# Where the last two spread groups are staged, and what the buffers of the dense expert part wait for

## The chip, the cores and the metric

The kernel runs on one core of a Trainium2 chip. The metric is the device time of one execution in microseconds (us); lower is better.

## The reference, cut to what matters

One decoder layer over 1,024 tokens of width 1,024: a mixer of three branches (stick-breaking attention, sparse attention, a gated recurrence), merged and added to x; then a PEER expert network; then a final norm. The expert network, of which the change touches a part, is:

```
h    = rms_norm(x)
s    = einsum(h @ w_q, sub_keys)           # 8 heads, two sets of 128 keys
top16 of each set -> 256 sums -> top16     # 128 of 16,384 experts per token
gate = softmax(best)
out  = sum over the 128: gate * gelu(h . u[e]) * v[e]
```

## The kernel before, in words

The tokens are worked on in four parts of 256 (`PARTS`). All parts go through the mixer, the merge, the output product (`wo`, lines 928 to 941), the second norm, the key scores and the routing. The experts are then computed in one of two ways.

Parts 0 and 3 are gathered (`gather_tile`, line 1139): for each tile of 128 tokens and each of 128 choices POOL issues an indirect DMA for one row of `u` (or `v`) per token, and DVE takes the dot product (line 1151) or adds the scaled row into the tile `gacc` (line 1161). Parts 1 and 2 (`DENSE`, 512 tokens) are computed densely: every one of the 16,384 experts for every token, with a matrix of gates that is zero where an expert was not chosen.

That matrix, `d_G`, is made by the spread pieces (`spread_pieces`, line 1208). Each call of `four` takes four tokens, a quad: DVE builds one-hot tiles `hot` (lines 1219 and 1220), PE multiplies them into a PSUM bank `gb` (lines 1223 and 1224, 8 matmuls a quad, two banks), and ACT evicts the 128x512 result into a staging tile (line 1226). After four quads, a group of 16 tokens, ACT issues the write of 1 MB into `d_G` (line 1228). There are 32 groups. Groups 0 to 29 go round three staging buffers: two halves of `stages` and one tile `stage` in the pool `per`; groups 30 and 31 use `stage` too, as group 29 does. `stages` shares its buffer with the tile `h2`, into which SP loads the normed tokens of the dense part (line 1389).

The dense part goes over 128 blocks of 128 experts. `gemm1` (line 1391) loads a block of `u` transposed (`uraw`, 512 KB, in a buffer of the pool `w4`, whose four buffers the `hot` tiles use as well), splits it into two fp16 parts (ACT line 220, DVE line 221, result `us`), makes 24 matmuls `g` (line 265) and a gelu on ACT into `ge` (line 1400, a buffer with the tag `at`). It runs three blocks ahead (`LEAD`). The main loop loads `vraw` (line 1422), and for every eight blocks two gate tiles `gt` (line 1429, 1 MB each, the first from groups 0 to 15 of `d_G`, the second from groups 16 to 31), multiplies `ge` by them (line 1434), splits the product into `ac`, and adds 18 matmuls into six PSUM banks `acc` (line 1441); a seventh and eighth sum lie in SBUF (`acc7`). Between the blocks it emits the pieces of part 3 that are left (`ending`): the rest of its output product, norm, scores and routing.

Pools: `per` and `w2` (SBUF) and `ps_z`, `ps_tr`, `ps_ov` (PSUM) belong to the mixer and are closed at line 1407. `late` (vraw, vs, gt, ac, acc7) and `ps_a` (acc) are opened after that (lines 1408 and 1409) over the same bytes and banks. With the default, `reuse_waits="pool"`, what is placed in a new pool waits until the pools that lay there are released as a whole. `w2` has the tags `sbk` (two buffers of 128x1024 fp32) and `sbv` (one), which hold keys and values of the stick-breaking attention (lines 385 and 396); the eight `at` buffers of 128x512 fp32 lie in `wk`, which stays open.

The order of the work: pieces are emitted in an order that a small planner in the kernel chooses (from line 1347: lists of pieces with dependencies, and work counts of PE and DVE). The framework then orders the instructions of each engine by priority and by a simulated timeline when the program is built, and sets all semaphores. At run time each engine and each DMA queue (SP's, ACT's, POOL's) goes through its list in order.

Of the kernel before, what the change touches and what calls it, by code (L numbers as in the profile page):

```python
# [10 lines left out]
F32 = mybir.dt.float32  # L11
# [5 lines left out]
AF = mybir.ActivationFunctionType  # L17
ALU = mybir.AluOpType
AX = mybir.AxisListType
PSUM = bass.MemoryType.PSUM  # L20
# [15 lines left out]
TH = 512  # L36
# [8 lines left out]
SGT, SA = 2.0 ** 10, 2.0 ** 4  # L45
# [26 lines left out]
def trunk(ctx: ExitStack, tc: tile.TileContext, a: dict, out: bass.AP):  # L72
    nc = tc.nc
    V, S, G, P = nc.vector, nc.scalar, nc.gpsimd, nc.tensor
# [13 lines left out]
    per = mix.enter_context(tc.tile_pool(name="per", bufs=1))  # L88
# [14 lines left out]
    def W4(name, shape=(128, 1024), dt=F32):  # L103
        return w4.tile(list(shape), dt, tag="w4", name=name)

    def W2(name, shape=(128, 512), dt=F32, tag="at", bufs=AT):
        return (wk if tag in ("at", "pre", "sg") else w2).tile(list(shape), dt, tag=tag, name=name, bufs=bufs)
# [98 lines left out]
    def dram(name, shape, dt=F32):  # L206
        return drm.tile(list(shape), dt, name=name)
# [92 lines left out]
    stages = hpl.tile([128, 2, 128, 16], F32, tag="h2", name="stages", bufs=1)  # L300
# [429 lines left out]
    def hg_pieces(h, pt, st):  # L730

        nm = f"hg{h}_{pt.i}"
        n = pt.n

        def pi():
            ps = proj(B_HI + h, hTs[pt.i], f"i_{nm}", pt)
            st["iT"] = PRE(f"iT_{nm}", pt)
            S.activation(st["iT"], ps, AF.Copy, scale=PS)

        def pi2():  # L740
            tr = transposed(st["iT"], f"i_{nm}", True)
            st["iv"] = W2(f"iv_{nm}", (128, n), tag="iv", bufs=2)
            S.activation(st["iv"], tr, AF.Copy)

        def pg(i, blk):
            if i == 0:
                st["raw"] = W2(f"raw_{nm}", (128, 3, n), tag="raw", bufs=2)
            ps = proj(blk + h, hTs[pt.i], f"r{i}_{nm}", pt)
            S.activation(st["raw"][:, i], ps, AF.Copy, scale=PS)

        return [pi, pi2, lambda: pg(0, B_HF), lambda: pg(1, B_HQ), lambda: pg(2, B_HG)]
# [126 lines left out]
    def gate_pieces(r, pt, st):  # L878

        def one(i):  # L880
            if i == 0:
                st["mg"] = W2(f"mg{r}_{pt.i}", (128, 6, pt.n), tag="mg", bufs=1)
            j, br = divmod(r * 6 + i, 3)
            ps = proj(B_MG + br * 8 + j, hTs[pt.i], f"mg{br}_{j}_{pt.i}", pt)
            S.activation(st["mg"][:, i], ps, AF.Copy, scale=PS)  # L885

        return [lambda i=i: one(i) for i in range(6)]
# [315 lines left out]
    d_G = dram("d_G", (32, 128, 128, 16))  # L1203
# [4 lines left out]
    def spread_pieces(pt):  # L1208

        stage = {}  # L1210

        def four(q):
            n0 = pt.t0 - TD + q * 4
            if q % 4 == 0:
                u = n0 // 16 % 3 if n0 < TH - 32 else 2
                stage[0] = per.tile([128, 128, 16], F32, tag="stage", name=f"stage{n0}") if u == 2 else stages[:, u]
            sp = spread[pt.i][:, :, q * 4:q * 4 + 4]
            hs = W4(f"hot{n0}", (128, 4, 128, 4), F16)
            V.tensor_tensor(hs[:, 0:2], iorep.unsqueeze(1).to_broadcast([128, 2, 128, 4]), sp[:, 0:2].unsqueeze(2).to_broadcast([128, 2, 128, 4]), op=ALU.is_equal)
            V.tensor_tensor(hs[:, 2:4], hs[:, 1:2].to_broadcast([128, 2, 128, 4]), sp[:, 2:4].unsqueeze(2).to_broadcast([128, 2, 128, 4]), op=ALU.mult)  # L1220
            ps = ps_mm.tile([128, 4, 128], F32, tag="mm", name=f"gb{n0}")
            for n in range(4):
                P.matmul(ps[:, n, :], hs[:, 0, :, n], hs[:, 2, :, n], start=True, stop=False)  # L1223
                P.matmul(ps[:, n, :], hs[:, 0, :, n], hs[:, 3, :, n], start=False, stop=True)
            m0 = q % 4 * 4
            S.activation(stage[0][:, :, m0:m0 + 4], ps.rearrange("p n i -> p i n"), AF.Copy, scale=SA / SGT)  # L1226
            if q % 4 == 3:
                nc.scalar.dma_start(d_G[n0 // 16], stage[0])

        return [lambda q=q: four(q) for q in range(pt.n // 4)]  # L1230

# [23 lines left out]
    def chain(fns, after=-100, before=1 << 30, deps=(), vector=False, to=None):  # L1255

        res = []
        for fn in fns:
            p = Piece(fn, after, before, list(deps) + res[-1:], vector)
            res.append(p)  # L1260
        (pieces if to is None else to).extend(res)
        return res

    def at(pt, r, kind, table, other=-10):
        i = pt.i * 4 + r
        return table.get((i // 4, i % 4, kind), other)
# [3 lines left out]
    for pt in PARTS:  # L1270
        i = pt.i
# [4 lines left out]
        for r in range(4):  # L1276
# [9 lines left out]
            p = chain(hg_pieces(r, pt, hg), ripe(at(pt, r - 2, "hg", end)), start[i, r, "hg"], here)  # L1286
            mg = None
            if r:
                mg = ({}, pt, r - 1)
                p = p + chain(gate_pieces(r - 1, pt, mg[0]), ripe(at(pt, r - 1, "hg", start)), start[i, r, "hg"], here)  # L1290
            elif i:
                prev = PARTS[i - 1]
                mg = (gates[i - 1], prev, 3)
                p = p + gates["p", i - 1]
            ng = state[i, "kv"] if r == 0 else None
            if ng is not None:
                p = p + kv[1:2]
# [49 lines left out]
    while t < N + 3 or todo:  # L1347
# [13 lines left out]
        for e, rate in (("DVE", RDVE), ("PE", RPE if t < N else REND)):  # L1361
# [5 lines left out]
            n = 0  # L1367
# [7 lines left out]
            while load_[e] < due[e]:  # L1375
                p = next((p for p in todo if not p.done and p.vector == (e == "DVE") and all(d.done for d in p.deps) and p.ready(t + 1)), None) if t < N or not n else None
# [28 lines left out]
    for k in range(LEAD):  # L1405
        ges[order[k]] = gemm1(order[k])
    mix.close()
    late = ctx.enter_context(tc.tile_pool(name="late", bufs=1))
    ps_a = ctx.enter_context(tc.tile_pool(name="ps_a", bufs=1, space=PSUM))
    accs = [ps_a.tile([128, 512], F32, name=f"acc{i}") for i in range(6)]  # L1410
    acc7 = late.tile([128, 2, 512], F32, name="acc7")
    V.memset(acc7, 0.0)
# [6 lines left out]
    for k, i in enumerate(order):  # L1419
# [23 lines left out]
        for u in range(6):  # L1443
            if u in (2, 4) and len(group) == 4:
                d0 = u // 2 - 1
                ps = ps_mm.tile([128, TH], F32, tag="mm", name=f"g2_{i}_{u}")
# [124 lines left out]
```

## Time and profile before

| | |
|---|---|
| time, median of 3 runs | 3502.78 us (3499.89 to 3507.8) |
| the profiled execution, device time | 3511.97 us |
| its span in the profile | 3510.2 us |
| PE busy | 3199.7 us |
| DVE busy | 3000.6 us |
| ACT busy | 1556.4 us |
| POOL busy | 1361.7 us |
| moved by DMA | 1058.00 MB |

Engines: PE multiplies, PEld loads its weights, DVE is the vector engine, ACT the scalar engine, POOL issues the gathers, SP most other DMAs. An instruction's row says what ended the idle time before it, in square brackets. A few matmul records can be missing, and their ends are modelled. The chain of waits follows the work that ended last back from its end, so a transfer stands there with the time for which it held that chain.

### The profile page before, as it was taken

The page shows a single profiled execution, that of the slowest core. Times are in us where ns is not written, and L with a number is a line of the kernel's source. Part 1 is how long each engine was busy: PE and PEld are TensorE (multiplying, and loading weights), DVE is VectorE, ACT ScalarE, POOL GpSimd, SP SyncE. Part 2 cuts the span into 40 slices and gives each one's busy share as a digit, 9 for nine tenths or more (in the row PEclk, how much of TensorE's full clock was granted, in tenths as well). Part 3 has the DMA queues.
Part 4 walks back from the last instruction along what each step waited for, and adds up shares of the span by engine and source line. Part 5 has one row for each costly group of instructions (what it writes and reads, how often), then busy time and mean ns, then how long its engine had stood idle before and what let it go on. Part 6 is the DMA issues. An engine that isn't in the chain of part 4 may idle for free.

```text
span 3510.2 us, 56907 instructions
## 1 busy us (share of the span) xinstructions
PE 3199.7 (91%) x20564; PEld 2175.3 (62%) x20564; DVE 3000.6 (85%) x6666; ACT 1556.4 (44%) x3181; POOL 1361.7 (39%) x1170
## 2 busy tenths in 40 slices
PE   7999889999997799999887889889999999999998
PEld 6887777778886688888565745434444444444443
DVE  6665679888789879889997869999988998998998
ACT  5776455554543554554455233333333333333333
POOL 0000002443332322333231334357765565676672
PEclk9999999999997799999688999989999999999999
DMA  8964856889976588897574998789999999999995
GB/s 305 334 248 147 308 185 226 320 314 310 358 284 231 199 289 291 327 332 259 191 250 154 344 372 312 241 271 387 392 384 329 385 367 362 362 368 375 367 358 219
DMA packets 359283, 1058.00 MB, mean 301 GB/s; under 512 B 35236, under 2 KB 107573, under 8 KB 354391
## 3 DMA queue, kind: packets, MB, share of 16 engines
q0 software_dynamic: 147456, 536.94, 42.5%
q1 hardware_dynamic: 206934, 483.87, 38.7%
q10 hardware_dynamic: 4608, 33.56, 2.5%
q8 instruction: 161, 2.64, 0.3%
q14 instruction: 124, 1.01, 0.1%
HBM read 944.13 MB, written 110.10 MB: 300 GB/s over the span
## 4 chain that ended last, share of the span: by engine, by line
PE 49%; DVE 23%; DMA 11%; issue 8%; ACT 6%; POOL 2%; SPq 0%; DVEq 0%; POOLq 0%; ACTq 0%
PE g L265 13%; PE acc L1441 10%; PE pj_mg L265 4%; DVE u L1151 3%; DVE gacc L1161 3%; PE g L1441 3%; DMA u<-in_peer_u_dram,gidx 3%; PE pj_r_hg L265 2%; DMA v<-in_peer_v_dram,gidx 1%; PE pb L265 1%; DMA gt<-d_G 1%; PE pj_wo L265 1%; POOL v L1159 1%; PE z_sb L417 1%; DMA vraw<-in_peer_v_dram 1%
## 5 line engine op out<-in xcount | busy, mean ns | idle before, releaser
L1159 POOL DMA_INDIRECT v<-in_peer_v_dram,gidx x421 | 556.0, 1321 | 674.0 <-DVE gacc L1161 348.4
L1149 POOL DMA_INDIRECT u<-in_peer_u_dram,gidx x417 | 529.7, 1270 | 596.6 <-DVE u L1151 367.4
L265 PE MATMUL g<-h,us 128*128 128x512 f16 x3072 | 688.2, 381 | 14.8 <-ACT ge L1400 12.1
L1441 PE MATMUL acc<-vs,ac 128*128 128x512 f16 x2304 | 542.2, 383 | 39.9 <-ACT vs L220 23.5
L1441 PEld LDWEIGHTS <-ac 128*128 128x128 f16 x3072 | 303.1, 99 | 426.1 <-issue 66.8
L1161 DVE SCALAR_TENSOR_TENSOR gacc<-v,act,gacc 128x1024 f32<-128x1024 f32 x421 | 538.9, 1280 | 29.4 <-DMA v<-in_peer_v_dram,gidx 25.8
L265 PEld LDWEIGHTS <-us 128*128 128x128 f16 x3072 | 301.6, 98 | 383.0 <-issue 21.1
L1151 DVE SCALAR_TENSOR_TENSOR u<-u,gh 128x1024 f32<-128x1024 f32 x417 | 501.9, 1219 | 33.2 <-DMA u<-in_peer_u_dram,gidx 32.7
L1400 ACT ACTIVATE ge<-g 128x512 f32<-128x512 f32 x128 | 76.1, 596 | 520.7 <-PE g L265 500.1
L265 PE MATMUL pj_mg<-hT,w_mg 128*128 128x256 f16 x2304 | 273.8, 275 | 4.0 <-ACT mg L885 4.0
L265 PEld LDWEIGHTS <-w_mg 128*128 128x128 f16 x2304 | 228.2, 100 | 33.6 <-issue 6.6
L1441 PE MATMUL g<-vs,ac 128*128 128x512 f16 x768 | 190.5, 388 | 11.6 <-ACT ge L1400 11.6
L1149 POOL DMA_INDIRECT rr_u<-in_peer_u_dram,gidx x95 | 134.2, 1413 | 96.7 <-DVE rr_u L1151 49.8
L221 DVE SCALAR_TENSOR_TENSOR vs<-vraw,vs 128x1024 f16<-128x1024 f32 x128 | 154.1, 1219 | 18.6 <-ACT vs L220 18.5
L221 DVE SCALAR_TENSOR_TENSOR us<-uraw,us 128x1024 f16<-128x1024 f32 x128 | 156.1, 1219 | 10.4 <-ACT us L220 10.3
L265 PE MATMUL pb<-o,w_b 128*128 128x256 f16 x1152 | 144.7, 281 | 21.1 <-DVE sg L923 15.1
L1159 POOL DMA_INDIRECT rr_v<-in_peer_v_dram,gidx x90 | 123.0, 1367 | 102.2 <-DVE gacc L1161 81.4
L220 ACT ACTIVATE vs<-vraw 128x1024 f16<-128x1024 f32 x128 | 131.0, 1046 | 55.0 <-DMA vraw<-in_peer_v_dram 55.0
L220 ACT ACTIVATE ac<-ge 128x512 f16<-128x512 f32 x128 | 79.9, 628 | 168.3 <-DVE ge L1434 139.0
L1434 DVE TENSOR_TENSOR ge<-ge,gt 128x256 f32<-128x256 f32 x256 | 98.4, 422 | 58.7 <-ACT ge L1400 44.9
L1223 PE MATMUL gb<-hot 128*128 128x128 f16 x512 | 125.7, 294 | 24.3 <-ACT stage L1226 13.1
L220 ACT ACTIVATE us<-uraw 128x1024 f16<-128x1024 f32 x128 | 134.2, 1048 | 21.4 <-PE g L265 12.8
(1146 smaller groups left out, 6353.8 us busy)
## 6 DMA issues: line engine op xcount, KB each, us to landing
uraw<-in_peer_uT_dram SPq DMA_DIRECT2D x128, 512.0 KB, 7.7
vraw<-in_peer_v_dram SPq DMA_DIRECT2D x128, 512.0 KB, 7.2
w_mg<-dw SPq DMA_DIRECT2D x72, 512.0 KB, 5.8
gt<-d_G SPq DMA_DIRECT2D x32, 1024.0 KB, 17.5
d_G<-stages ACTq DMA_DIRECT2D x20, 1024.0 KB, 5.9
w_r_hg<-dw SPq DMA_DIRECT2D x36, 512.0 KB, 5.4
w_b<-dw SPq DMA_DIRECT2D x72, 256.0 KB, 5.5
wr_mg<-in_wblk_dram SPq DMA_DIRECT2D x24, 512.0 KB, 5.3
```

The lines of the kernel that those rows point to most:

```text
L220: S.activation(hi, src, AF.Copy, scale=scale)
L221: V.scalar_tensor_tensor(lo, in0=src, scalar=scale, in1=hi, op0=ALU.mult, op1=ALU.subtract)
L265: P.matmul(ps, l[:, k, :], r[:, k, :], start=(i == 0), stop=(i == n - 1))
L417: P.matmul(x["z"], qz[:, hh, tl * 128:(tl + 1) * 128], st["k"][:, r0 + c0:r0 + c1], start=True, stop=(c0 > 0))
L1149: G.indirect_dma_start(out=ur, out_offset=None, in_=a["peer_u"], in_offset=bass.IndirectOffsetOnAxis(ap=idx[:, c:c + 1], axis=0))
L1151: V.scalar_tensor_tensor(ur, in0=ur, scalar=1.0, in1=h2, op0=ALU.mult, op1=ALU.mult, accum_out=hpre[:, c:c + 1])
L1159: G.indirect_dma_start(out=vr, out_offset=None, in_=a["peer_v"], in_offset=bass.IndirectOffsetOnAxis(ap=idx[:, c:c + 1], axis=0))
L1161: V.scalar_tensor_tensor(acc, in0=vr, scalar=act[:, c:c + 1], in1=acc, op0=ALU.mult, op1=ALU.add)
L1223: P.matmul(ps[:, n, :], hs[:, 0, :, n], hs[:, 2, :, n], start=True, stop=False)
L1400: S.activation(ge, ps, AF.Gelu, scale=1.0 / (SW * SH2))
L1434: V.tensor_tensor(gv, gv, gt[:, :, i % 8, :], op=ALU.mult)
L1441: P.matmul(ps, ac[:, x, t * 128:(t + 1) * 128], v[:, y, dh * 512:(dh + 1) * 512], start=start and n == 0, stop=stop and n == 2)
```

## The change

Group 30 is staged in two tiles of the tag `sbk` (64 of the 128 columns of experts in each), group 31 in one tile of the tag `sbv` (64 columns) and two of the tag `at` (32 each). A quad's eviction and a group's write to `d_G` are made once for each tile, so two times for group 30 and three times for group 31. Groups 0 to 29 are staged as before. The pools `late` and `ps_a` are opened with `reuse_waits="tile"`: each of their tiles waits only for those tiles of the closed pools that used its own bytes or banks.

```diff
             if q % 4 == 0:
-                u = n0 // 16 % 3 if n0 < TH - 32 else 2
-                stage[0] = per.tile([128, 128, 16], F32, tag="stage", name=f"stage{n0}") if u == 2 else stages[:, u]
+                u = n0 // 16 % 3
+                if n0 < TH - 32:
+                    stage[0] = [per.tile([128, 128, 16], F32, tag="stage", name=f"stage{n0}") if u == 2 else stages[:, u]]
+                elif n0 < TH - 16:
+                    stage[0] = [W2(f"stage{n0}_{i}", (128, 64, 16), tag="sbk", bufs=2) for i in range(2)]
+                else:
+                    stage[0] = [W2(f"stage{n0}", (128, 64, 16), tag="sbv", bufs=1)] + [W2(f"stage{n0}_{i}", (128, 32, 16)) for i in range(2)]
...
             m0 = q % 4 * 4
-            S.activation(stage[0][:, :, m0:m0 + 4], ps.rearrange("p n i -> p i n"), AF.Copy, scale=SA / SGT)
-            if q % 4 == 3:
-                nc.scalar.dma_start(d_G[n0 // 16], stage[0])
+            i0 = 0
+            for s in stage[0]:
+                i1 = i0 + s.shape[1]
+                S.activation(s[:, :, m0:m0 + 4], ps[:, :, i0:i1].rearrange("p n i -> p i n"), AF.Copy, scale=SA / SGT)
+                if q % 4 == 3:
+                    nc.scalar.dma_start(d_G[n0 // 16][:, i0:i1], s)
+                i0 = i1
...
     mix.close()
-    late = ctx.enter_context(tc.tile_pool(name="late", bufs=1))
-    ps_a = ctx.enter_context(tc.tile_pool(name="ps_a", bufs=1, space=PSUM))
+    late = ctx.enter_context(tc.tile_pool(name="late", bufs=1, reuse_waits="tile"))
+    ps_a = ctx.enter_context(tc.tile_pool(name="ps_a", bufs=1, space=PSUM, reuse_waits="tile"))
```

## Rows read from the trace of the kernel before

**Rows 1.** The page's busy time of each engine, share of the span, instructions.

```profile
PE 3199.7 (91%) x20564; PEld 2175.3 (62%) x20564; DVE 3000.6 (85%) x6666; ACT 1556.4 (44%) x3181; POOL 1361.7 (39%) x1170
```

**Rows 2.** Stretches: length, busy us of PE, PEld, DVE, ACT, POOL, PEclk, DMA share, GB/s.

```profile
2012.00:2016.00 4.00, 4.00 (x38) 3.72 (x36) 4.00 (x8) 0.98 (x2) 2.30 (x1) 1.00 0.74 232
2016.00:2020.00 4.00, 0.91 (x8) 0.72 (x7) 4.00 (x7) 0.00 (x0) 3.34 (x2) 0.80 0.94 334
2020.00:2024.00 4.00, 0.00 (x0) 0.00 (x0) 3.04 (x4) 0.00 (x0) 2.69 (x3) 0.50 1.01 421
...
2044.00:2048.00 4.00, 4.00 (x20) 1.81 (x19) 1.35 (x2) 1.06 (x1) 2.79 (x2) 1.00 1.02 423
2048.00:2074.00 26.00, 22.10 (x114) 11.00 (x112) 16.07 (x23) 8.34 (x11) 7.94 (x5) 1.00 1.07 371
...
2082.00:3486.00 1404.00, 1340.74 (x6236) 616.60 (x6235) 1295.24 (x2071) 464.59 (x618) 853.15 (x602) 0.98 0.95 347
```

**Rows 3.** Timeline of ACT and its queue: start, duration, instruction, idle time before.

```profile
2015.06 0.39 ACT L935 ACTIVATE y<-pj_wo 128x256 f32<-128x256 f32 x1 [2.02 <-PE pj_wo L265]
2024.21 1.09 ACT L1226 ACTIVATE stage<-gb 128x512 f32<-128x512 f32 x2 [8.76 <-DMA d_G<-stage]
...
2034.00 1.09 ACT L1226 ACTIVATE stage<-gb 128x512 f32<-128x512 f32 x2 [3.13 <-DMA d_G<-stage]
...
2037.23 1.05 ACT L220 ACTIVATE us<-uraw 128x1024 f16<-128x1024 f32 x1
2037.37 0.33 ACTq L1228 DMA_DIRECT2D d_G<-stage  x1
```

**Rows 4.** Timeline of PE around the change.

```profile
2012.22 2.80 PE L265 MATMUL pj_wo<-m,w_wo 128*128 128x256 f16 x24
...
2024.86 0.28 PE L1223 MATMUL gb<-hot 128*128 128x128 f16 x1 [7.94 <-ACT stage L1226]
...
2026.74 3.72 PE L265 MATMUL pj_wo<-m,w_wo 128*128 128x256 f16 x24
...
2034.65 0.28 PE L1223 MATMUL gb<-hot 128*128 128x128 f16 x1 [2.30 <-ACT stage L1226]
...
2039.59 11.43 PE L265 MATMUL g<-h,us 128*128 128x512 f16 x46 [0.22 <-DVE us L221]
2052.04 10.52 PE L265 MATMUL g<-h,us 128*128 128x512 f16 x48 [1.02 <-ACT ge L1400]
```

**Rows 5.** Timeline of DVE: the last one-hot tiles, groups of neighbouring instructions merged.

```profile
2025.49 1.29 DVE L1161 SCALAR_TENSOR_TENSOR gacc<-v,act,gacc 128x1024 f32<-128x1024 f32 x1 [2.46 <-DMA v<-in_peer_v_dram,gidx]
2026.70 1.29 DVE L1219 TENSOR_TENSOR hot<-iorep,spread 128x1024 f16<-128x1024 f16 x2
2027.90 1.29 DVE L1220 TENSOR_TENSOR hot<-hot,spread 128x1024 f16<-128x1024 f16 x2
```

**Rows 6.** The page's DMA issues: count, KB each, median us from issue to landing.

```profile
d_G<-stages ACTq DMA_DIRECT2D x20, 1024.0 KB, 5.9
...
w_b<-dw SPq DMA_DIRECT2D x72, 256.0 KB, 5.5
```

**Rows 7.** The same for ACT's issue between 2037 and 2038, the last group's write.

```profile
d_G<-stage ACTq DMA_DIRECT2D x1, 1024.0 KB, 10.1
```

**Rows 8.** Timeline of SP's queue, from two stretches.

```profile
2031.43 4.68 SPq L100 DMA_DIRECT2D uraw<-in_peer_uT_dram  x3
...
2050.16 1.54 SPq L100 DMA_DIRECT2D uraw<-in_peer_uT_dram  x2
...
2052.22 11.87 SPq L1429 DMA_DIRECT2D gt<-d_G  x2
```

**Rows 9.** The chain that ended last, its two longest transfers after 2030.

```profile
2036.73 12.27 DMA uraw<-in_peer_uT_dram
...
2052.70 20.25 DMA gt<-d_G
```

**Rows 10.** All DMA traffic from 2010 to 2074.

```profile
DMA packets 10011, 23.11 MB, mean 361 GB/s; under 512 B 579, under 2 KB 5656, under 8 KB 9362
```

## The prediction

> **What bounds the kernel now.** I began with the busy times of the page: PE is busy 91% of the span and DVE 85% [rows 1]. Neither is slack enough to ignore, and a mean over 3.5 ms says nothing about a change that touches one place. That place is where the spread pieces end and the dense part begins, so I next cut the span into stretches [rows 2]. [...] The DMA engines, 0.74 busy from 2012 to 2016, are full from then on: shares of 0.94 to 1.07, up to 421 and 423 GB/s. And after 2082 PE is busy 1340.74 of 1404 us (95%) and DVE 1295.24 (92%): from there to the end the kernel runs at PE's pace, with DVE and the DMA engines (0.95) close behind. So an earlier start of the dense part should move the end, if those two let it.
>
> [...] ACT's timeline: it does nothing for 8.76 us before the eviction at 2024.21 and for 3.13 us before the one at 2034.00, both times until the transfer d_G<-stage has landed [rows 3]. Groups 29, 30 and 31 share the one buffer `stage`, so a group's first eviction waits for the write of the group before. PE's timeline shows the same holes one step later: 7.94 and 2.30 us in front of a spread matmul, released by ACT [rows 4].
>
> **The change, part by part.** The sum is made against the profiled execution, 3511.97 us on the device for a span of 3510.2. That is 9.2 us above the median of the runs shown, 3502.78; what I take off it in us I take off the median too.
>
> *Group 30 in two `sbk` buffers, group 31 in `sbv` and two `at` buffers.* Neither group waits for a write any more, since the stick-breaking tiles that last filled those buffers are long read. The upper bound is PE's two holes: 7.94 + 2.30 = 10.2 us [rows 4]. The lower bound comes from DVE, which must build the one-hots first. In the order that DVE has now, the last two L1219 stand behind a gacc at 2025.49 that itself waited 2.46 us for its gathered row; their products start at 2027.90 and take 0.7 us each, so the second-last quad cannot start before 2028.6 [rows 5]. It starts at 2034.65 now [rows 4], which makes 6.05 us. The order may be laid anew, since the two slots come free earlier, but a gathered row that lands late stays a fact of full DMA engines. I take 7.5, nearer to DVE's end; both ends are kept.
>
> *More evictions and more writes.* A quad of group 30 takes two evictions of 128x256 in place of one of 128x512: 2 x 0.39 against 1.09 / 2 = 0.55 [rows 3], so +0.23, four times 0.9 us. One of group 31 takes one of 128x256 and two of 128x128. For the last kind I have no row here and put it between half of 0.39 and all of it: +0.23 to +0.62 a quad, 0.9 to 2.5 in all. Three more DMA issues of 0.33 add 1 us to ACT's queue [rows 3]. That is 2.8 to 4.4 us on an engine that sat idle for 8.76, and most of it lies beside PE's matmuls, which have two PSUM buffers to run ahead in. Bare is only the last quad's part and the issues behind it, ahead of the first split of `us` on ACT. I take 0.5 us of loss; ends 0 and 4.4. The bytes stay 1 MB a group. A 1 MB write landed after 5.9 us in the median and a 256 KB load after 5.5 [rows 6], so smaller pieces in flight together are costed at nothing; the cover is that they leave one right behind the other. Without it, the two further pieces of group 31 would bring 2 x 5.5 us, in front of a gt load alone.
>
> *The clock.* With PE idle, the wo product took 3.72 us at 2026.74 against 2.80 at 2012.22, and 46 g matmuls took 11.43 us where 48 later took 10.52 (so 46 would take 10.08) [rows 4]: 0.92 + 1.35 = 2.3 us. If all idle time goes, so does that; if DVE keeps PE waiting it may stay. I take 1.5; ends 0 and 2.3.
>
> *`late` waits tile by tile.* Its first users are the vraw and gt loads on SP's queue and the memset of acc7. Group 31's write left at 2037.37 [rows 3] and took 10.1 us to land [rows 7], until 2047.5, so the pool as a whole could open no earlier. But SP has its own reason to be late: two uraw loads stand ahead at 2050.16, whose buffers DVE must first split, and the gt loads follow at 2052.22 [rows 8]. The second gt load reads groups 16 to 31 and needs the last write in any case. I cost this part at nothing; what covers it is SP's order. A gain is bounded by what PE loses up to the first acc matmul, 26.00 - 22.10 = 3.9 us from 2048 to 2074 [rows 2]; a loss under the second rival.
>
> *`ps_a` waits bank by bank.* Nothing: the chain into the first acc matmul runs through a gt load of 20.25 us that lands at 2072.95, not through a bank [rows 9].
>
> *The ceiling.* The same bytes must still pass. From 2010 to 2074, 64 us, 23.11 MB moved [rows 10]; at the 423 GB/s of the best stretch [rows 2] they take 54.6 us, so no more than 9.4 us can go unless gathers are put off.
>
> Sum: 7.5 - 0.5 + 1.5 + 0 = 8.5 us, just under the ceiling. 3511.97 becomes 3503.5, the median 3502.78 becomes **3494.3**. The forecast's own range has 6.05 - 4.4 + 0 = 1.7 us at the small end and the ceiling's 9.4 at the large one: 3493 to 3501.
>
> **The rivals.**
>
> *The full DMA engines take it back.* Asked for 8 us sooner, the uraw loads meet the same gathers and land later. For: the shares near 1 from 2016 on [rows 2]; and the fourth uraw load took 12.27 us [rows 9], while the first had landed when its split began at 2037.23 [rows 3], 5.8 us after its issue at 2031.43 [rows 8]. Against: the engines were at 0.74 just before. If the first load too takes 12.27, then 6.5 of the 8.5 us are gone: 3500.8, no difference that can be told. [...]
>
> *SP's queue (slower).* With less to wait for in `late`, a gt load may be laid on SP ahead of the fourth uraw load, and SP works in order. The last pieces of group 31 would leave 6 us earlier, near 2031.4, and land 10.1 us later [rows 7], at 2041.5; the issue of two gt loads took 11.87 us, of the second alone 11.4 [rows 8]; so the fourth uraw would leave at 2052.9 instead of 2036.73, land at 2065.2, and after 1.05 us on ACT [rows 3] and as much on DVE PE could start the fourth block at 2067.3. It now runs the third and fourth from 2052.04 in 10.52 us, thus starts the fourth at 2057.3 [rows 4]. Loss 10.0 us: 3512.8. It decides when a gt load stands on SP before the fourth uraw. For: SP's first uraw leaves only at 2031.43 [rows 8], and a builder that sees free buffers may put other loads in front. Against: gt's data come late, and the uraw loads are asked for first.
>
> *More than the sum.* All holes and the slow clock go, the first acc matmul stops waiting, and gathers are put off, which lifts the ceiling: 10.2 + 2.3 + 3.9 = 16.4 us, 3486.4. For: the order of every engine is written anew when the program is built, that of the gathers included. Against: nothing in the change asks for it.
>
> *The second half does nothing.* Where bytes and order hold the loads anyway, the new waits change no instruction; that is in the forecast's sum already, at nothing.
>
> **How the numbers follow.** A measurement of this kernel can tell about 0.2%, 7 us, so faster means under 3495.8. The forecast gets 0.44 (0.30 under that line, where its point lies, 0.14 within), more than the sum 0.18, the DMA engines 0.22 (within), SP's queue 0.16. Faster 0.30 + 0.18 = 0.48, same 0.14 + 0.22 = 0.36, slower 0.16. The range goes from 3484, under the large gain with a little for the runs' own spread, to 3511, which leaves out the worse half of SP's case and a little on both sides: about 2 in 10.
>
> **What the next profile should show.** Right: ACT no longer waits on d_G<-stage at L1226, PE's hole of 7.94 us is gone, its clock stays near 1.00 from 2016 to 2036, and the first acc matmul comes 6 to 12 us earlier than at 2074. DVE's wait for a gathered row becomes the longest of that stretch. Wrong by the DMA rival: the holes go, but ACT's split of `us` waits for uraw by as much. Wrong by SP: a gt issue above the fourth uraw. And if the first acc matmul is earlier but the end is not, then the stretch after 2082 was not PE's alone, and DVE's share there, 92% now, goes up.

## The result, and the profile after

The changed kernel takes 3522.24 us (median of 7 runs, 3516.31 to 3540.18), the kernel before 3503.95 us beside it (7 runs, 3499.89 to 3509.45): a ratio of 1.006, 95% interval 1.0037 to 1.0082. It is slower by 0.6%, some 21 us by that ratio, where the prediction said 8.5 us faster.

The stage waits are gone all the same. ACT's timeline of the changed kernel at the last two groups (start, duration, instruction, idle time before it; L1234 is now the eviction):

```profile
2002.38 0.33 ACTq L1236 DMA_DIRECT2D d_G<-stage  x1
...
2005.31 0.66 ACT L1234 ACTIVATE stage<-gb 128x256 f32<-128x256 f32 x2 [0.55 <-PE gb L1229]
...
2012.99 0.72 ACT L1234 ACTIVATE stage<-gb 128x256 f32<-128x256 f32 x3 [0.56 <-PE gb L1229]
...
2020.83 1.06 ACT L220 ACTIVATE us<-uraw 128x1024 f16<-128x1024 f32 x1 [4.07 <-DMA uraw<-in_peer_uT_dram]
2025.49 1.06 ACT L220 ACTIVATE us<-uraw 128x1024 f16<-128x1024 f32 x1 [3.60 <-DMA uraw<-in_peer_uT_dram]
```

No eviction waits for a write of `d_G` any more; the waits of 8.76 and 3.13 us [rows 3] are replaced by waits for `uraw` in front of the splits. The first line, the issue of group 29's write, is the last event that both kernels have in common: up to the last one-hots the traces show the same order of instructions on every engine. Times below count from it (2013.06 in the trace before, 2002.38 here; over the traces of all these experiments it lies between 1997.0 and 2017.8, so that difference is spread between runs). By that count the first acc matmul comes after 51.1 us instead of 61.1, and the program ends after 1512.1 instead of 1497.1. So the dense part starts 10 us earlier, and 25 us are lost behind that.

Three stretches show where: from group 29's write to the first acc matmul, to that of block 9, to that of block 18. The kernel before (length, busy us of PE, PEld, DVE, ACT, POOL, PEclk, DMA share, GB/s):

```profile
2013.10:2074.20 61.10, 44.92 (x255) 26.50 (x254) 40.17 (x50) 16.94 (x25) 25.19 (x16) 0.86 1.01 367
2074.20:2177.20 103.00, 100.47 (x557) 55.68 (x558) 88.10 (x191) 41.96 (x61) 40.10 (x31) 1.00 0.93 328
2177.20:2319.30 142.10, 119.44 (x544) 56.20 (x542) 138.01 (x428) 40.37 (x52) 58.92 (x41) 0.92 0.76 249
```

The changed kernel, same columns:

```profile
2002.40:2053.50 51.10, 36.89 (x205) 21.16 (x203) 33.46 (x43) 16.78 (x35) 20.54 (x12) 0.84 1.03 383
2053.50:2176.00 122.50, 114.06 (x606) 62.01 (x607) 98.34 (x201) 40.29 (x61) 43.58 (x38) 0.95 0.91 312
2176.00:2321.50 145.50, 119.00 (x545) 56.43 (x544) 139.05 (x429) 40.54 (x53) 57.44 (x42) 0.89 0.76 247
```

Three readings. **The 10 us are no saved time**: 205 matmuls stand before the first acc matmul instead of 255. The block of `g` and the wo product that ran ahead of it now run behind it (606 in the second stretch instead of 557). The 255th matmul after the write of group 29 starts at 61.7 us here and at 61.6 before. DVE, too, has done four gathered rows fewer. **The clock did not come back** either: 0.84 in the first stretch where it was 0.86. **And behind block 9 DVE is busy 138.01 of 142.10 us before the change (97%), PE 119.44 (84%).** So PE has more idle time there than DVE, and the stretch need not run at PE's pace.

Next come the engines in the second stretch, which takes 19.5 us more than before. PE's timeline of the changed kernel at block 0:

```profile
2053.49 6.19 PE L1450 MATMUL acc<-vs,ac 128*128 128x512 f16 x18 [4.93 <-ACT ac L220]
2059.52 2.78 PE L265 MATMUL pj_wo<-m,w_wo 128*128 128x256 f16 x24
2062.14 0.38 PE L282 MATMUL tr_wo<-packed,y 128*128 128x128 f32 x2
```

DVE's timeline, at the same place and at block 8:

```profile
2052.30 1.43 DVE L1443 TENSOR_TENSOR ge<-ge,gt 128x256 f32<-128x256 f32 x4 [2.86 <-DMA gt<-d_G]
...
2062.56 0.48 DVE L941 TENSOR_TENSOR x<-x,tr_wo 128x128 f32<-128x128 f32 x2 [5.28 <-PE tr_wo L282]
...
2137.91 0.42 DVE L1443 TENSOR_TENSOR ge<-ge,gt 128x256 f32<-128x256 f32 x1 [6.54 <-DMA gt<-d_G]
```

SP's queue in the changed kernel:

```profile
2012.99 18.30 SPq L100 DMA_DIRECT2D uraw<-in_peer_uT_dram  x7
2031.34 0.42 SPq L100 DMA_DIRECT2D vraw<-in_peer_v_dram  x1
2031.82 8.06 SPq L1438 DMA_DIRECT2D gt<-d_G  x2
2039.97 7.04 SPq L100 DMA_DIRECT2D vraw<-in_peer_v_dram  x1
2047.10 1.25 SPq L255 DMA_DIRECT2D w_wo<-dw  x1
```

and in the kernel before, ahead of the uraw loads at 2050.16 [rows 8]:

```profile
2045.87 0.33 SPq L255 DMA_DIRECT2D w_wo<-dw  x1
```

The load of part 3's next weights, `w_wo`, is now behind the first gt loads and two vraw loads; before, it stood ahead of the seventh uraw. PE waits 4.93 us for block 0's `ac` with the wo product behind that, and DVE waits 5.28 us for the wo product with its gathered rows behind that. In these waits neither engine takes up what stands behind in its list, and the lists had been laid anew.

### The profile page after: what moved, and what is told of

Read it like the earlier page. It is cut to its first block, busy times and chain, and to the rows that moved or that the text cites. A ratio compares the mean times of both kernels' runs of the same rounds, so it can differ in the third digit from the quotient of the medians.

```text
span 3514.5 us, 56947 instructions
## 1 busy us (share of the span) xinstructions
PE 3188.4 (91%) x20564; PEld 2166.2 (62%) x20564; DVE 2998.8 (85%) x6666; ACT 1550.6 (44%) x3190; POOL 1334.6 (38%) x1170
## 5 line engine op out<-in xcount | busy, mean ns | idle before, releaser
L1159 POOL DMA_INDIRECT v<-in_peer_v_dram,gidx x421 | 531.9, 1263 | 699.2 <-DVE gacc L1161 399.9
L1149 POOL DMA_INDIRECT u<-in_peer_u_dram,gidx x417 | 520.8, 1249 | 633.3 <-DVE u L1151 389.9
L265 PE MATMUL g<-h,us 128*128 128x512 f16 x3072 | 695.7, 384 | 31.5 <-ACT ge L1409 11.5
L265 PEld LDWEIGHTS <-us 128*128 128x128 f16 x3072 | 303.1, 99 | 404.5 <-issue 35.9
L1149 POOL DMA_INDIRECT rr_u<-in_peer_u_dram,gidx x95 | 143.4, 1509 | 75.0 <-DVE rr_u L1151 44.6
L265 PE MATMUL pj_r_hg<-hT,w_r_hg 128*128 128x256 f16 x1152 | 138.9, 278 | 3.8 <-ACT raw_hg L749 3.5
```

The costliest lines, as they stand in the source:

```text
L265: P.matmul(ps, l[:, k, :], r[:, k, :], start=(i == 0), stop=(i == n - 1))
L1149: G.indirect_dma_start(out=ur, out_offset=None, in_=a["peer_u"], in_offset=bass.IndirectOffsetOnAxis(ap=idx[:, c:c + 1], axis=0))
L1159: G.indirect_dma_start(out=vr, out_offset=None, in_=a["peer_v"], in_offset=bass.IndirectOffsetOnAxis(ap=idx[:, c:c + 1], axis=0))
```

## The experiments

Theory A: the loss lies in the lists that the build lays for the new buffers. Theory B: it lies in the finer waits of `late` and `ps_a`. Theory C: an earlier start on full DMA engines costs at run time, whatever the lists. In the table, start of the first acc matmul of blocks 0, 9, 18 and 72 and the end, us after group 29's write, from one trace each; ratios are of the timed runs to those of the kernel before on the same chip.

| run | 0 | 9 | 18 | 72 | end | ratio (95% interval) |
|---|---|---|---|---|---|---|
| before | 61.1 | 164.1 | 306.3 | 894.2 | 1497.1 | |
| changed | 51.1 | 173.7 | 319.1 | 913.9 | 1512.1 | 1.0060 (1.0037 to 1.0082) |
| e1_stage | 51.3 | 171.7 | 318.3 | 923.2 | 1526.4 | 1.0058 (1.0037 to 1.0079) |
| e2_waits | 61.5 | 166.1 | 311.8 | 901.5 | 1495.5 | 1.0001 (0.9986 to 1.0015) |
| e3_one | 52.5 | 172.7 | 317.8 | 913.0 | 1515.9 | 1.0042 (1.0026 to 1.0057) |
| e4_gathers | 51.1 | 171.8 | 314.1 | 912.3 | 1514.4 | 1.0039 (1.0020 to 1.0057) |
| f1_before_lists | 60.1 | 163.3 | 305.4 | 895.0 | 1490.6 | 0.9984 (0.9971 to 0.9998) |
| f12_lists_again | 60.5 | 163.4 | 308.2 | 898.9 | 1491.4 | 0.9987 (0.9974 to 1.0000) |
| f2_after_lists | 56.4 | 180.1 | 325.7 | 930.6 | 1532.1 | 1.0088 (1.0064 to 1.0112) |
| f3_dve_list | 70.8 | 173.3 | 314.6 | 907.7 | 1517.7 | 1.0055 (1.0036 to 1.0075) |
| f4_sp_list | 53.6 | 157.0 | 299.3 | 894.0 | 1504.0 | 1.0031 (1.0019 to 1.0044) |
| f5_sp_and_late | 54.1 | 157.3 | 303.1 | 894.7 | 1496.7 | 0.9993 (0.9978 to 1.0008) |
| f6_six_pieces | 51.9 | 174.7 | 318.0 | 909.0 | 1511.4 | 1.0058 (1.0042 to 1.0073) |
| f7_three_pieces | 53.8 | 157.7 | 303.8 | 901.9 | 1502.4 | 1.0008 (0.9994 to 1.0022) |
| f8_gt_ahead | 50.9 | 173.0 | 318.2 | 916.8 | 1517.8 | 1.0059 (1.0039 to 1.0080) |
| f10_dve_more | 60.0 | 163.0 | 311.7 | 904.2 | 1501.7 | 1.0022 (1.0009 to 1.0035) |
| f11_pe_more | 58.4 | 161.5 | 308.9 | 897.5 | 1496.9 | 0.9997 (0.9983 to 1.0012) |

**Halves of the change.** e1 has the staging alone, e2 the finer waits alone, e3 both but moves only group 30.

```diff
 e1_stage: the changed kernel, but
-    late = ctx.enter_context(tc.tile_pool(name="late", bufs=1, reuse_waits="tile"))
-    ps_a = ctx.enter_context(tc.tile_pool(name="ps_a", bufs=1, space=PSUM, reuse_waits="tile"))
+    late = ctx.enter_context(tc.tile_pool(name="late", bufs=1))
+    ps_a = ctx.enter_context(tc.tile_pool(name="ps_a", bufs=1, space=PSUM))
 e2_waits: the kernel before, with the two lines marked - here in place of those marked +
 e3_one: the changed kernel, but
-                if n0 < TH - 32:
+                if n0 < TH - 32 or n0 >= TH - 16:
...
-if u == 2 else stages[:, u]]
+if u == 2 or n0 >= TH - 16 else stages[:, u]]
```

> Only the staging of groups 30 and 31 is changed; late and ps_a wait pool by pool as before. The instruction lists of all five engines come out the same as those of the changed kernel, and five waits differ. Theory A (the loss lies in the lists that the build lays after the spread stage): the changed kernel's time, 3516 to 3528 us. Theory B (the loss lies in late's tile-wise waits, which let gt and vraw loads go earlier onto full DMA engines): the waits are back, so 3490 to 3500 us.

> Only reuse_waits="tile" for late and ps_a; groups 30 and 31 stay in the tile stage. All five lists come out the same as before the change; five waits differ. Theory A: 3500 to 3508 us, no difference from before. Theory B: slower than before by 10 to 20 us.

> As the changed kernel, but only group 30 is staged in the two sbk buffers; group 31 goes back to the tile stage, which group 29's write has left by then. ACT's wait of 8.76 us goes all the same, so the first acc matmul should come as early as in the changed kernel, within 3 us. The lists of the dense part come out different again: as many gathers ahead of blocks 12 to 66 as in the changed kernel, but as many as before the change ahead of blocks 78 to 126. Theory A: another time than the changed kernel's 3522, between 3500 and 3518 us. Theory C (an early start on full DMA engines costs time at run time, whatever the lists): 3518 to 3526 us.

e1 is as slow as the whole change, e2 as fast as the kernel before: the finer waits change nothing that can be told, and in the traces no engine's order differs with or without them. Theory B falls. One moved group is enough for most of the loss. Between A and C e3 decides nothing: its 3525.39 us lie in the range expected for C, but the kernel before took 3510.59 us beside it, and its ratio puts it at 3518.7 on the scale of the first runs, on the line between the two.

**Where the gathers stand.** e4 lays the gathers' arithmetic of the first 40 dense blocks behind the block that it followed in the kernel before.

```diff
 in paced(), with NB the counts of gathers ahead of each block's ac in the list before
-        return tc.issue_after(paces[min(k, len(paces) - 2)])
+        j = bisect.bisect_right(NB, k) - 1
+        return tc.issue_after(paces[min(k, len(paces) - 2)] if j < 0 else dacs[j])
```

> The changed kernel, with one thing added: each gathered row's DVE instruction from number 422 on may not be laid ahead of the dense block's ac split that it followed in the kernel before (for the first 40 blocks). The count of gathers ahead of each block then is that of the kernel before within 3 up to block 108, instead of up to 7 more. Theory A, in the form that the surplus gathers on DVE hold the dense blocks: the gain of the transition shows at the end, 3490 to 3500 us. Theory C: 3516 to 3526 us. If it lies near 3505, the gathers' places are half of it and something else in the lists is the rest.

It lies between the two, and its interval overlaps that of the changed kernel: the places of the gathers are at most a part of the loss, and theory A in this form falls.

**The lists held.** To try A against C the lists were held whole: for each engine an edge from every instruction to the one that follows it in the wanted list, from the last spread groups on. Such an edge sets issue order alone. In f1's trace PE, DVE, POOL and SP go through exactly the order that they had in the kernel before, and ACT differs by the new evictions and writes alone.

```diff
+    for e, (first, data) in ORDER.items():
+        q = np.cumsum(np.frombuffer(zlib.decompress(base64.b85decode(data)), np.int16).astype(int))
+        for x, y in zip(q[first:], q[first + 1:]):
+            tc.add_manual_dep(lists[e][y], lists[e][x].name, mybir.DependencyInfo(mybir.DependencyClass.NoSync, mybir.DependencyReason.DATA), reason="order")
```

> The changed kernel with its new buffers and its finer waits, but every engine's list from the last spread groups on is held, by edges that set issue order alone, to the order that the kernel before had (each old eviction is replaced by its new ones, each write by its new ones). Theory A, the loss lies in the lists that the build lays for the new buffers: the transition still gains some 8 to 10 us between group 29's write and the first acc matmul and the loss between blocks 6 and 9 is gone, so the end is 4 to 10 us before that of the kernel before: ratio 0.997 to 0.999, about 3495 to 3500 us where the kernel before has 3504 to 3510. Theory A', the gain is real but work behind it takes it back whatever the list (the engines wait for the same loads): ratio 0.999 to 1.001. Theory C, starting the dense part early on full DMA engines costs by itself: ratio 1.003 or above, as the changed kernel.

> The kernel before, with its old stage buffers and its waits for whole pools, but with every engine's list from the last spread groups on held to the order that the changed kernel has. Theory A: the lists carry the loss without any of the new buffers, and the old waits add theirs: ratio 1.004 to 1.009 against the kernel before, acc block 9 at 180 us or more behind group 29's write (164 in the kernel before, 174 in the changed one). Theory C: with the old waits the dense part starts as late as before, so the loss goes away: ratio 0.999 to 1.002.

> The run with all lists held to the order of the kernel before, once more, beside the two that add work to it. Theory: the removed waits themselves are worth a little, ratio 0.997 to 0.9995 as in the first time. Rival: nothing, 0.9995 to 1.001.

This settles the sign. New buffers with the old lists: 0.9984, and 0.9987 when repeated, some 4 to 6 us faster. Old buffers with the new lists: 1.0088. The lists cost 0.7 to 0.9% with either buffers. The buffers themselves are worth 0.1 to 0.3%, hardly beyond the noise: f12's interval ends at 1.0000, and those of the changed kernel and f2 overlap. Theory A holds. C is not tried by these runs, since f1's dense part starts hardly earlier than before and f2's starts 4.7 us earlier in spite of the old waits. It falls with f5 and f7 below: their first acc matmuls come 7.0 and 7.3 us earlier, and they lose nothing that can be told. f1 is the fastest version found.

But f1 also shows that the gain forecast for the transition is not there: its first acc matmul comes 1.0 us earlier than before, not 8.5. Its three stretches:

```profile
2001.10:2061.20 60.10, 47.71 (x255) 26.77 (x252) 39.89 (x50) 18.41 (x38) 22.51 (x16) 0.83 1.02 377
2061.20:2164.40 103.20, 100.52 (x558) 55.76 (x558) 88.12 (x191) 42.01 (x61) 40.19 (x31) 1.00 0.93 327
2164.40:2306.50 142.10, 119.80 (x544) 56.35 (x542) 136.94 (x421) 40.38 (x52) 57.87 (x41) 0.92 0.76 248
```

DVE's idle time in the first is 20.2 us as against 20.9. PE's idle time falls from 16.2 us to 12.4, but its 255 matmuls take 47.71 us where they took 44.92, at a granted clock of 0.83 for 0.86. PE's waits in that stretch (engine, line, what it waited for: us in total, times, longest), the kernel before:

```profile
PE gb L1223 <- ACT stage L1226: 10.2, 2, 7.9
...
PE g L265 <- ACT us L220: 1.6, 1, 1.6
...
PE g L265 <- DVE us L221: 0.2, 1, 0.2
```

and f1:

```profile
PE g L269 <- ACT us L224: 4.8, 2, 3.3
PE gb L1232 <- DVE hot L1229: 4.2, 2, 3.3
PE g L269 <- DVE us L225: 2.6, 1, 2.6
```

The 10.2 us behind the stage buffer have become 4.2 behind the one-hots, and the waits for the split of `us` have grown from 1.8 to 7.4 us. Little of that is a late uraw load, as f1's timelines of ACT and of DVE show:

```profile
2021.37 0.33 ACTq L1240 DMA_DIRECT2D d_G<-stage  x1
2021.74 1.06 ACT L224 ACTIVATE us<-uraw 128x1024 f16<-128x1024 f32 x1 [0.40 <-ACT stage L1238]
2024.27 1.06 ACT L224 ACTIVATE us<-uraw 128x1024 f16<-128x1024 f32 x1 [1.47 <-DMA uraw<-in_peer_uT_dram]
```

```profile
2026.57 1.28 DVE L1165 SCALAR_TENSOR_TENSOR gacc<-v,act,gacc 128x1024 f32<-128x1024 f32 x1 [2.70 <-DMA v<-in_peer_v_dram,gidx]
2027.77 2.35 DVE L225 SCALAR_TENSOR_TENSOR us<-uraw,us 128x1024 f16<-128x1024 f32 x2
```

PE's first 3.3 us pass while ACT works through the last evictions and writes to its first split, 1.5 stand behind a uraw load, and 2.6 behind DVE, whose old list has a gathered row in front of its splits. DVE waited 2.70 us for that row. The fourth uraw load left 5.2 us earlier than before, by the count from group 29's write, and took 11.4 us where it had taken 12.27 [rows 9]. It was the gathered rows that came late. POOL issued two of them 8.4 and 10.2 us after group 29's write in both kernels; their median time to landing in the kernel before and in f1:

```profile
v<-in_peer_v_dram,gidx POOLq DMA_INDIRECT x2, 7.4
v<-in_peer_v_dram,gidx POOLq DMA_INDIRECT x2, 10.8
```

In f1 the DMA engines stand at a share of 1.02, and the uraw loads, asked for earlier, are under way at the same time.

**One list at a time.** The other lists are laid by the build round the one that is held, so these runs are less clean.

> The changed kernel with DVE's list alone held to the order that the kernel before had; the other engines' lists are laid by the build round it. If the loss comes of where the gathers' arithmetic and part 3's norm and top-k steps stand among the dense part's work on DVE, this has all that the run with all lists has: ratio within 0.001 of it. If it comes of the order of loads on SP (gt_0, gt_16 and vraw ahead of part 3's w_wo loads, which this build still has), it stays at 1.003 or above.

> The changed kernel with SP's list alone held to the order that the kernel before had (w_wo ahead of uraw6, vraw0 and gt); the other lists are laid by the build round it, and DVE's differs from that of the kernel before by only 2 to 4 gathers at a block. If SP's order of loads is what holds part 3's chain back, the loss is gone: ratio 0.997 to 1.001. If the places on DVE decide, it stays between 1.002 and 1.006.

With DVE's old list alone the first acc matmul comes after 70.8 us: DVE in its old order waits 15.5 us for a wo product, whose weights SP still loads late. Its 1.0055 shows that DVE's order alone does not mend the loss. With SP's old list alone the early loss is gone, though the ratio, 1.0031, lies where it was expected if the places on DVE decide. Block 9 starts 7.1 us earlier than in the kernel before, with 255 matmuls ahead of the first acc again. That lead is 7.0 us at block 18 and 4.5 at block 66, and is lost behind that, where this build laid the gathers otherwise (between blocks 90 and 96, 39 gathered rows in 84.3 us; before, 35 in 72.6).

> The changed kernel with SP's list held to the order that the kernel before had, and the lists of PE, ACT and DVE held to that order only from dense block 18 on; ahead of block 18 they are laid by the build, as in the run with SP's list alone. Theory A: up to block 18 this is the run with SP's list alone (acc block 18 some 299 us behind group 29's write, 306 in the kernel before), and from there it takes the 1164 to 1191 us that the kernel before and the run with all lists held took from block 18 to the end: ratio 0.995 to 0.998, the fastest so far. Rival: the late loss of the run with SP's list alone comes of the earlier start itself (what is gained ahead is waited for later), then the ratio stays at 1.001 to 1.004.

f5 keeps that front and takes the old lists from block 18 on. The lead goes from 6.8 us at block 9 to 3.2 at block 18, and is gone at block 36 (508.7 against 508.1). At the first acc matmul f5 had done 419 gathered rows and the kernel before 423; at block 18 both had done 493. Four rows at 1.28 us each are some 5 us of DVE's time, so what looked like a lead was mostly DVE work put off. Neither theory's number came: 0.9993, no difference.

**Single causes.** Two edits of the source, and one of a held list, each mend a thing that the traces named.

```diff
 f6_six_pieces (f7_three_pieces: 3 for 6)
+    for _ in range(6):
+        ending.pop(0).emit(1 << 20)
     mix.close()
...
-    gone = 0
+    gone = 6
 f8_gt_ahead: all lists held as the changed kernel has them, but on SP
-... vraw9 vraw10 w_pq18 vraw11 gt gt ...
+... vraw9 gt gt vraw10 w_pq18 vraw11 ...
```

> The changed kernel with one edit in its source: the next six pieces of part 3's tail (its w_wo products 5 to 7 and the additions between them) are written ahead of dense block 0 and no longer between blocks 0 and 1. The build then lays w_wo21 ahead of uraw6, vraw0 and gt_0 on SP, w_wo22 behind them, and the gathers stand within 5 of the places that they had in the kernel before. Theory A (part 3's chain held back by SP's order is the loss): block 6 to 9 takes about 51 us as before and not 67, ratio 0.996 to 1.000. Rival (any list but the old one loses): ratio 1.003 or above.

> As the run with six pieces, with only three of them written ahead of dense block 0. SP's order is then almost that of the kernel before (w_wo21 ahead of uraw6; uraw7 behind gt_01), but from block 72 on the gathers stand 6 to 17 places behind those of the kernel before, most at blocks 108 to 126. Theory A, first half (SP's order): up to block 66 it is at or ahead of the kernel before, counted from group 29's write. Second half (late gathers leave DVE work for the end, where PE then waits): the last 18 blocks take 10 to 20 us more than the 180 to 200 of the kernel before: ratio 1.001 to 1.006. If late gathers cost nothing: 0.996 to 1.000.

> The changed kernel with every engine's list held to its own order, with one edit: on SP the fourth gt load (block 8's second half) and the fifth are moved ahead of vraw10, w_pq18 and vraw11, where the kernel before has them. In the changed kernel DVE waits 6.5 us for that load at block 8, with its gathers and part 3's top-k steps queued behind. Theory G, that wait is a main piece of the loss: block 6 to 9 takes 58 to 63 us and not 67, the end comes 4 to 7 us earlier, ratio 1.003 to 1.005 where the changed kernel has 1.006. Rival: the load is late because block 7 frees its buffer late, not because of the queue; then nothing moves, ratio 1.005 to 1.007.

f8 is the cleanest, and the theory fails: the wait goes and the time stays. DVE's waits from the first acc to block 18, the changed kernel:

```profile
DVE ge L1443 <- DMA gt<-d_G: 12.1, 2, 6.5
DVE x L941 <- PE tr_wo L282: 5.7, 2, 5.3
DVE gacc L1161 <- DMA v<-in_peer_v_dram,gidx: 4.3, 6, 1.1
DVE ge L1443 <- ACT ge L1409: 4.3, 3, 3.0
```

and f8:

```profile
DVE ge L1447 <- ACT ge L1413: 11.8, 5, 6.3
DVE gacc L1165 <- DMA v<-in_peer_v_dram,gidx: 7.3, 4, 4.1
DVE x L945 <- PE tr_wo L286: 4.9, 2, 4.5
...
DVE ge L1447 <- DMA gt<-d_G: 1.1, 1, 1.1
```

12.1 us of waiting for gt became 1.1, and waiting for ACT and for gathered rows took its place. f6 has `w_wo` in its old place and loses as before, so that single load isn't the cause either. f7 does not lose early: PE has 248 matmuls ahead of its first acc, near the old 252, where f6 has 204 and the changed kernel 202 (counted by their starts; a window's count takes in those that straddle its edges). Its gathers fall behind later (984 rows done at block 120 instead of 1010), yet it comes out at 1.0008; that late gathers cost 10 to 20 us is not borne out.

All runs that lose between blocks 0 and 9 (changed, e1, e3, e4, f2, f6, f8) have PE's first acc ahead of some 50 matmuls that used to precede it, and no other run has. That is a correlation over lists that differ in other places too. PE's new order with SP's old one was not tried; there, by argument, uraw loads would stand ahead of gt on SP while their buffers wait for matmuls behind the acc on PE.

**Whose pace?** f10 and f11 take f1 and add about the same time to one engine, in blocks 9 to 18. f11's additions go into one of its sums, so that sum is no longer the layer's.

```diff
 f10_dve_more, behind the split of ac
+        if 9 <= k < 19:
+            for _ in range(3):
+                V.scalar_tensor_tensor(pad, in0=ge[:, 0:256], scalar=1.0, in1=ge[:, 256:512], op0=ALU.mult, op1=ALU.mult)
 f11_pe_more, behind the loop over u
+        if 9 <= k < 19:
+            for _ in range(2):
+                gemm2(accs[5], 2, 1, ac, v, False, False)
```

> The run with all lists held to the order of the kernel before, plus work for DVE alone that nobody uses: in each of blocks 9 to 18, behind the split of ac, three products of 128x256 into a spare buffer, some 0.42 us each, 12.6 us in all. If DVE sets the pace of this stage (138.01 us busy of 142.10 between acc block 9 and 18 in the kernel before, PE 119.44), block 9 to 18 takes 10 to 13 us more, and the end comes 8 to 13 us later than in the run without: ratio 1.001 to 1.002 where that has 0.998. If PE sets it, as the prediction had it, less than 4 us.

> The run with all lists held to the order of the kernel before, plus work for PE alone: in each of blocks 9 to 18 the last six acc products (accumulator 5, both orders of the two-part product) are issued twice more as one set of six, 60 matmuls of 128x512, some 0.215 us each, 12.9 us in all; accumulator 5 counts these blocks twice to three times over, so the output of that part is changed. If PE sets the pace of the stage from the first acc on, as the prediction had it, block 9 to 18 and the end take 10 to 13 us more: ratio 1.001 to 1.003. If DVE sets it there, 0 to 4 us at block 18: ratio 0.998 to 0.9995.

Against f12 on the same chip (3501.80 us), 12.7 us of DVE work (30 at 0.424 us) bring 10.0 us at the end (3511.80), and 60 matmuls more on PE, 12.9 us by the estimate of 0.215 each (in the trace before, 24 `g` matmuls of that shape start at 2087.83 and the acc behind them at 2093.01, 0.216 each), bring 2.5 (3504.34). From block 9 to 18, f12 (columns as above):

```profile
2171.70:2316.50 144.80, 120.02 (x544) 56.19 (x543) 137.23 (x423) 40.38 (x52) 58.10 (x41) 0.91 0.74 243
```

f10, with more for DVE:

```profile
2169.30:2318.00 148.70, 120.72 (x544) 56.66 (x543) 146.49 (x445) 40.50 (x53) 53.69 (x40) 0.91 0.73 237
```

f11, with more for PE:

```profile
2165.70:2313.10 147.40, 127.29 (x599) 60.91 (x597) 138.73 (x428) 41.75 (x53) 58.81 (x41) 0.94 0.74 242
```

DVE's busy time rises by 9.3 us and leaves 2.2 us idle; PE's rises by 7.3, less than what was added, and its granted clock from 0.91 to 0.94. f12 took 144.8 us there and f1 142.1, so within this stretch alone the traces spread too much to tell the two apart. The timed runs do: the intervals of f10 (1.0009 to 1.0035) and f12 (0.9974 to 1.0000) do not meet, those of f11 and f12 overlap widely. f10's and f11's own overlap a little; their medians lie 7.5 us apart. So work added right behind the transition costs the end when it is DVE's, and hardly when it is PE's. Where it is paid is not shown: of f10's 10.0 us its trace has 3.9 by block 18, and f11's has 2.6 there.

## Why the prediction was wrong

**Two steps failed, and the first lost the sign.** Every term of the sum priced the old lists with shorter waits. That the order is laid anew stands in the prediction at nothing: "The order may be laid anew" in the first term, and in the third rival "nothing in the change asks for it". f1, f12 and f2 show in its place that the re-laid lists cost 0.7 to 0.9%, some 26 to 31 us, with either buffers, while the new buffers on the old lists gain 4 to 6 us.

The second step is in the first part: "from there to the end the kernel runs at PE's pace", "So an earlier start of the dense part should move the end". It rests on one row over 1404 us [rows 2], PE 95% and DVE 92%. That mean hides the stretch right behind the transition, blocks 9 to 18, where DVE is at 97% and PE at 84%. f10 and f11 show that DVE's work counts there and PE's hardly does, and f5 that a lead of 6.8 us at block 9 is gone at block 36. The prediction had its own test for this, a first acc matmul that comes earlier with an end that does not, and it came true. Its second half did not: DVE's share from 2082 to 3486 is 91% in the changed kernel, not above 92%, because waits came with the work.

**The stage waits, 7.5 us.** They went, as said. On the old lists (f1) the one-hots put 4.2 of the 10.2 us back, so 6.0 are gone: the low end that the prediction took from DVE's order, 6.05. Of these 6.0 only 1.0 is left at the first acc. That full DMA engines take it back was the first rival, with 0.22 and 2 us left of 8.5, but it named the wrong load. In f1 the fourth uraw load was no slower than before (11.4 us for 12.27); the gathered rows were (10.8 us for 7.4), and DVE's splits stand behind them. In the changed kernel, where that load left 10.0 us earlier, it did take longer, 15.7 us for 12.27. That SP's loads, leaving earlier, held POOL's rows up is the author's reading of these numbers; no run shows which transfer yields.

**The clock, 1.5 us.** Not gained: PEclk was 0.86 up to the first acc before, 0.84 after, 0.83 in f1. PE still waits, only for something else, and the same 255 matmuls took 2.8 us more in f1 than before: a loss where a gain was forecast. That the clock comes back as the idle time goes was the author's estimate; in f1 PE's idle time fell from 16.2 to 12.4 us, and the clock did not rise.

**More evictions and writes, 0.5 us.** The evictions themselves were sized well: 0.28 us for one of 128x128, 0.66 for two of 128x256. What lies bare is more than 0.5: between the last spread matmul and the first `g`, PE waits 3.29 us in f1 where it waited 1.63, so 1.7 us, within the prediction's ends of 0 and 4.4. The smaller writes were costed at nothing. In the changed kernel they landed after 8.2 us for 512 KB and 12.7 for 256 KB in the median of the few that were timed, against 10.1 for the 1 MB of group 31 before [rows 7]; the cover, that they leave one right behind the other, holds in f1 (group 31's three issues start 0.68 us apart), and no run prices them alone.

**The second half at nothing.** Right: e2 is at 1.0001.

**The slower rival** had SP's queue in mind, but at another load: the first four uraw went first, at 2012.99, and it was part 3's `w_wo` that the gt loads passed. So its condition did not come, and a time on its side of the forecast is no support for its mechanism. f4 shows that SP's order, and what the build lays round it, carries the early loss; f6 and f8 show that neither `w_wo` alone nor the fourth gt load alone does.

**What stays open.** Which difference of the new lists costs the 10 us by which block 9 starts late, and where in f1 the last 4 to 6 us are gained: its trace runs level with the one before to block 72 (895.0 against 894.2), and the later differences lie in stretches where e2, with no new buffers, differs as well.

## What to carry to other kernels

Before a gain is passed on to the end, read the busy shares of the stretch right behind it, not of the whole remainder, and add a little work to one engine at a time to see which the end pays for. Where the order is laid by a scheduler at build time, a change of buffers is also a change of every list behind it. Compare the lists first, and hold the old ones to price the buffers alone. And an earlier milestone is a gain only if as much work lies in front of it: count the matmuls and rows done by then.

## What was not expected of the hardware

With the same lists, stretches of the dense part repeat almost to the tenth: blocks 24 to 30, 36 to 42, 42 to 48 and 48 to 54 took 59.6, 60.9, 71.4 and 51.6 us in the traces of the kernel before, e2 and f1 alike, while the changed kernel's list took 60.5, 60.7, 68.0 and 56.3. In these stretches a difference of up to 4.7 us came with another list; blocks 18 to 36 as a whole took 201.9, 203.5 and 203.5 us with the same. And part of the work added to PE cost no busy time: with 55 more matmul records in blocks 9 to 18 (599 for 544) PE was busy 7.3 us more, and the granted clock there was 0.94 in place of 0.91.
